# Gate products for eight tokens at a time, gate stores issued by ScalarE, a paired comparison in decoding, and weight tiles that begin 52 bytes in

## The chip, the cores and the metric

The kernel runs on one core of one Trainium2 chip. The metric is the device time of one execution in microseconds (us); a kernel's time is the median over its runs. The core has five engines that work side by side: TensorE (PE; PEld is its loading of weights), VectorE (DVE), ScalarE (ACT), GpSimd (POOL) and SyncE (SP, which only issues transfers here).

## The reference, cut to what matters

The reference is a whole network in fp32, with 256 tokens of 1,024 features. A first block of two layers (SwiGLU, a mixer of three recurrences, SwiGLU) is followed by a second block of two layers (attention, then PEER), with a second stream of 256 context tokens that is needed in its first layer only. PEER is the part that the change touches by its code:

```python
def peer(h, w_q, sub_keys, u, v):            # 8 heads, 128 keys, top 16, 16384 experts
    q = (h @ w_q).reshape(T, 8, 2, 128)
    s = jnp.einsum('thpd,hpnd->thpn', q, sub_keys)
    sv, si = lax.top_k(s, 16)
    cand = (sv[:, :, 0, :, None] + sv[:, :, 1, None, :]).reshape(T, 8, 256)
    fv, fi = lax.top_k(cand, 16)
    i1 = jnp.take_along_axis(si[:, :, 0], fi // 16, axis=-1)
    i2 = jnp.take_along_axis(si[:, :, 1], fi % 16, axis=-1)
    g = jax.nn.softmax(fv, axis=-1)
    # each token: sum over its 128 chosen experts of g * gelu(h . u[i]) * v[i],  i = i1 * 128 + i2
```

It runs three times: on the tokens and on the context in layer 0, and on the tokens in layer 1. Outside of it nearly all the work is matrix products of the 256 tokens with weights.

## The kernel before

**Matrix products.** Every fp32 product is made of three faster ones (mm3, L242): each operand is split into a high part H and a rest L, and H x H, H x L and L x H are added up in PSUM. wsplit (L229) splits each weight tile that a transfer has brought into raw or rawx: split (L214) lets ScalarE copy H (L221), VectorE subtract to L (L224), and GpSimd subtract a share of it (L226). The tiles wh, wl (wxh, wxl, wch, wcl in other pools) are 1,024 + 64 floats long on each partition, and the split weights lie in them from float LEAD on (L220; LEAD is 16, 64 bytes). In the two expert functions it is 0 where the tokens are 512 at a time. The weights are the operand that TensorE loads (128 x 128), the tokens are streamed through (256 columns, or 512).

**PEER.** A sparse choice of experts is computed densely: all 16,384 experts are applied to all tokens, and a gate matrix with zeros for what wasn't chosen multiplies the activations. route_choices makes the queries and the top 16. route_gates (L1330) then works on two blocks of 128 tokens. decode (L1349) turns the 128 choices of each token into key numbers i1 and i2 and gates: it finds the two ranks ra and rb by arithmetic, compares each with 0 to 15 into eq (tag req, L1381, 2,048 elements), multiplies by the list of keys (L1384), adds up in halves (L1386, L1388), and transposes. gates (L1402) builds the matrix: for four tokens VectorE compares key numbers with 0 to 127 into e (g_e, L1412, 1,024 elements) and multiplies its first half by three bf16 parts of the gate into o (g_o, L1416, 1,536 elements); twelve bf16 matmuls fill one PSUM bank r, ScalarE copies it into rst (L1424), and after eight such steps SP issues the store of 2 MB to the DRAM buffer gd (L1425). One place makes 8 stores; there are three places, so 24. g_e and g_o have three buffers each, r has two banks, rst two buffers.

**Around it.** The three places lie beside other work: the context's beside a SwiGLU (about 1270 to 1512 us), the tokens' of layer 0 beside the first nine groups of the context's experts (1820 to 2040), and those of layer 1 beside the first groups of its own experts (3527 to 3709). An expert group is hidden (products with u, GELU, tag act), and some groups later (15 at the third place) down: gated loads the gates back from gd into eG (L1461), VectorE multiplies them into ea (L1465) and splits it (eah, eal), and products with v are added up in acc. Behind the second place the pools change: rawx and wx are opened and the experts run 512 tokens at a time.

**Order.** The order on each engine is fixed when the kernel is built, by a scheduler that goes by its own estimates; on the chip each engine works in that order and waits on semaphores. SP issues the loads of weights and, up to now, the stores of gates, in one order (L197 is a load of raw or rawx).

Of the kernel before, what the change touches and what calls it, by code (L numbers as in the profile page):

```python
# [15 lines left out]
U32 = mybir.dt.uint32  # L16
U8 = mybir.dt.uint8
BF = mybir.dt.bfloat16
AF = mybir.ActivationFunctionType
OP = mybir.AluOpType  # L20
# [9 lines left out]
GD_LEVELS = (2, 4, 8, 16, 32, 64)  # L30
NFIRST = 9

LEAD = 16


TIERS = ((0, 0, 1, 16), (16, 1, 3, 8), (40, 4, 4, 4), (56, 8, 8, 1))
# [72 lines left out]
class Net:  # L109
    def __init__(self, ctx, tc):  # L110
# [9 lines left out]
        self.mod, self.mw = {}, {}  # L120
        self.nsplit, self.share, self.pooled, self.ngap, self.lead = 0, 0, 0, 0, LEAD

# [1207 lines left out]
    def route_gates(self, choices, gd, base, side="left"):  # L1330
        stack, si, fv, fi = choices
        with stack, self.route_pool("b", side) as self.ph, self.psum("routeb", side, r=2):
            self.gb = dict(e=3, o=3)
            iota2 = self.t([128, 128, 2], "iota2", 1, BF)
            self.nc.gpsimd.tensor_copy(iota2, self.c("iota").unsqueeze(2).to_broadcast([128, 128, 2]))
            for tb in range(2):
                jt = self.decode(si[tb], fv[tb], fi[tb])
                self.gates(jt, iota2, gd, base + tb * 4)
# [10 lines left out]
    def decode(self, si, fv, fi):  # L1349


        nc = self.nc
        e = self.t([128, 8, 16], "rge")
        z = self.t([128, 8], "rgz")
        nc.vector.tensor_tensor(e, fv, fv[:, :, 0:1].to_broadcast([128, 8, 16]), OP.subtract)
        nc.scalar.activation(e, e, AF.Exp)
        nc.vector.tensor_reduce(z, e, AX.X, OP.add)
        nc.vector.reciprocal(z, z)
        nc.vector.tensor_tensor(e, e, z.unsqueeze(2).to_broadcast([128, 8, 16]), OP.mult)
        sif = self.t([128, 8, 2, 16], "rsif", 1, BF)  # L1360
        nc.vector.tensor_copy(sif.rearrange("p h a k -> p (h a) k"), si)

        sh = self.t([128, 8, 16], "rsh", 1, U32)
        nc.vector.tensor_scalar(sh, fi, 3, None, OP.logical_shift_right)
        p, ra, rb, x = [self.t([128, 8, 16], f"rr{i}", 1, BF) for i in range(4)]
        nc.vector.tensor_copy(p, fi)
        nc.vector.tensor_scalar(ra, sh, -1.0, 0.0, OP.add, OP.max)
        sh = self.t([128, 8, 16], "rsh", 1, U32)
        nc.vector.tensor_scalar(sh, fi, 2, None, OP.logical_shift_right)
        nc.vector.scalar_tensor_tensor(ra, sh, -6.0, ra, OP.add, OP.max)  # L1370
        nc.vector.scalar_tensor_tensor(ra, p, -48.0, ra, OP.add, OP.max)
        nc.vector.tensor_scalar(x, ra, 8.0, 8.0, OP.mult, OP.add)
        nc.vector.scalar_tensor_tensor(x, ra, 16.0, x, OP.mult, OP.min)
        nc.vector.tensor_scalar(rb, ra, 4.0, 24.0, OP.mult, OP.add)
        nc.vector.tensor_tensor(x, x, rb, OP.min)
        nc.vector.scalar_tensor_tensor(x, ra, 48.0, x, OP.add, OP.min)
        nc.vector.tensor_tensor(rb, p, x, OP.subtract)
        tp = self.bank((128, 3, 128), "r")
        for i, r in enumerate((ra, rb)):
            eq = self.t([128, 128, 16], "req", 1, BF)  # L1380
            nc.vector.tensor_tensor(eq, r.rearrange("p h k -> p (h k)").unsqueeze(2).to_broadcast([128, 128, 16]),  # L1381
                                    self.iota16.unsqueeze(1).to_broadcast([128, 128, 16]), OP.is_equal)
            e4 = eq.rearrange("p (h k) a -> p h k a", h=8)
            nc.vector.tensor_tensor(e4, e4, sif[:, :, i].unsqueeze(2).to_broadcast([128, 8, 16, 16]), OP.mult)  # L1384
            for n in (8, 4, 2):
                nc.vector.tensor_tensor(eq[:, :, 0:n], eq[:, :, 0:n], eq[:, :, n:2 * n], OP.add)  # L1386
            ii = self.t([128, 128], "rii")
            nc.vector.tensor_tensor(ii, eq[:, :, 0], eq[:, :, 1], OP.add)  # L1388
            nc.tensor.transpose(tp[:, i], ii, self.ident)
        nc.tensor.transpose(tp[:, 2], e.rearrange("p h k -> p (h k)"), self.ident)  # L1390
        ji = self.t([128, 64, 2, 2], "rji", 2, BF)
        jg = self.t([128, 64, 3, 2], "rjg", 2, BF)
        nc.scalar.copy(ji.rearrange("p n c t -> p c n t"), tp[:, 0:2].rearrange("p c (n t) -> p c n t", t=2))
        g = tp[:, 2].rearrange("p (n t) -> p n t", t=2)
        nc.vector.tensor_copy(jg[:, :, 0], g)
        g1 = self.t([128, 64, 2], "rg")
        nc.vector.tensor_tensor(g1, g, jg[:, :, 0], OP.subtract)
        nc.vector.tensor_copy(jg[:, :, 1], g1)
        nc.vector.tensor_tensor(jg[:, :, 2], g1, jg[:, :, 1], OP.subtract)
        return ji, jg  # L1400

    def gates(self, j, iota2, gd, base):  # L1402

        nc = self.nc
        ji, jg = j
        for c in range(4):
            st = self.t([128, 128, 32], "rst", 2)
            for q in range(8):
                n0 = c * 16 + q * 2
                e = self.g([128, 2, 2, 128, 2], "e", BF)  # L1410
                o = self.g([128, 2, 3, 128, 2], "o", BF)
                nc.vector.tensor_tensor(e.rearrange("p n c i t -> p (n c) i t"),  # L1412
                                        iota2.unsqueeze(1).to_broadcast([128, 4, 128, 2]),
                                        ji[:, n0:n0 + 2].rearrange("p n c t -> p (n c) t").unsqueeze(2)
                                        .to_broadcast([128, 4, 128, 2]), OP.is_equal)
                nc.vector.tensor_tensor(o, e[:, :, 0:1].to_broadcast([128, 2, 3, 128, 2]),  # L1416
                                        jg[:, n0:n0 + 2].unsqueeze(3).to_broadcast([128, 2, 3, 128, 2]), OP.mult)
                ps = self.bank((128, 4, 128), "r")
                for t in range(4):
                    l, r = e[:, t // 2, 1, :, t % 2], o[:, t // 2, :, :, t % 2]  # L1420
                    for i in range(3):
                        self.mm(ps[:, t], l, r[:, i], t + i == 0, t == 3 and i == 2)
                dst = st.rearrange("p i t -> p t i")[:, q * 4:q * 4 + 4]
                nc.scalar.copy(dst, ps)  # L1424
            nc.sync.dma_start(gd[base + c], st.rearrange("p i t -> p (i t)"))  # L1425

    def experts(self, h, grps, u_d, v_d, gd, f=None, quiet=()):

# [12 lines left out]
        def hidden(grp):  # L1441
            self.lead = 0 if T == 512 else LEAD
            acts[grp] = []
# [26 lines left out]
        def down(grp):  # L1470
            As = gated(grp)
            self.lead = 0 if T == 512 else LEAD
            for half in range(2):
# [28 lines left out]
        for grp in grps[-lag:] if lag else ():  # L1502
            down(grp)
        self.share, self.lead = 0, LEAD
        return acc
# [282 lines left out]
```

## Time and profile before

| | us |
|---|---|
| median of 3 runs | 4281.34 |
| lowest and highest | 4268.89, 4295.14 |
| the profiled execution | 4265.51 |
| its span, first to last instruction | 4263.7 |
| TensorE busy in it | 4092.1 |
| VectorE busy in it | 2884.7 |
| ScalarE busy in it | 1948.4 |
| GpSimd busy in it | 1404.4 |

Busy times are those of the profile's page. Matmuls are pipelined: one of 256 columns lasts about 0.28 us from its start to its modelled end, while the next starts after 0.11 to 0.12 us, so the pace is read from starts, or as a stretch's length divided by its matmuls. The granted clock (PEclk) is a share of full speed. A name such as g_o<-g_e,rjg is the tile written and the tiles read, and L1416 the line of the kernel.

### The profile page before, as it was taken

What the parts mean: (1) busy time and instruction counts of PE and PEld (TensorE: products, weight loads), DVE (VectorE), ACT (ScalarE), POOL (GpSimd) and SP (SyncE); (2) the same over time, 40 slices, a digit from 0 to 9 for tenths busy, and PEclk for the clock granted to TensorE, in tenths of its full rate; (3) what the DMA queues carried; (4) which work ended last, traced back from release to release, by engine and by line L of the source; (5) the groups of instructions that cost most, each with busy time, mean ns of one, the idle gap of its engine ahead of it and who ended that gap; (6) DMA issues with size and microseconds to landing.
All of it is one profiled execution on the core that took longest, in us unless ns stands there. A gap on an engine that the chain in (4) does not pass through costs nothing.

```text
span 4263.7 us, 77051 instructions
## 1 busy us (share of the span) xinstructions
PE 4092.1 (96%) x31290; PEld 3779.8 (89%) x31290; DVE 2884.7 (68%) x5472; ACT 1948.4 (46%) x2711; POOL 1404.4 (33%) x1239
## 2 busy tenths in 40 slices
PE   8999999999999999999899999999999999899999
PEld 8998999998979987999688888888998699799999
DVE  6686757786869966999444444444656789775555
ACT  4462555444535644556332332323444546644443
POOL 5641454555402200420222222222354131005554
PEclk9999999999999989999999999999999999999999
DMA  6545654545365552456434333333464135686654
GB/s 213 179 165 203 228 174 154 187 140 191 135 232 188 208 184 87 169 198 228 168 119 129 113 125 119 124 114 120 162 213 159 74 132 200 250 279 209 216 193 143
DMA packets 174995, 727.43 MB, mean 171 GB/s; under 512 B 12080, under 2 KB 87088, under 8 KB 103856
## 3 DMA queue, kind: packets, MB, share of 16 engines
q1 hardware_dynamic: 174640, 722.52, 48.5%
q8 instruction: 245, 4.01, 0.4%
q14 instruction: 110, 0.90, 0.1%
HBM read 668.99 MB, written 53.48 MB: 169 GB/s over the span
## 4 chain that ended last, share of the span: by engine, by line
PE 83%; DVE 12%; issue 2%; DMA 1%; ACT 1%; POOL 1%; SPq 0%; DVEq 0%; ACTq 0%; POOLq 0%
PE acc L240 29%; PE act L240 23%; PE pj L240 21%; PE r L240 3%; PE gd L240 2%; DVE wl L224 2%; PE s L240 1%; PE hg L240 1%; DVE wcl L224 1%; PE o L240 1%; DVE g_o L1416 1%; PE pt L991 1%; PE at L240 1%; ACT wh L221 1%; DVE g_e L1412 1%
## 5 line engine op out<-in xcount | busy, mean ns | idle before, releaser
L226 POOL TENSOR_TENSOR wl<-raw,wh 128x256 fp32r<-128x256 f32 (+2 forms) x419 | 595.6, 1423 | 1377.2 <-ACT wh L221 1347.1
L221 ACT CAST wh<-raw 128x1024 fp32r<-128x1024 f32 x592 | 620.8, 1051 | 730.5 <-PE acc L240 315.8
L224 DVE TENSOR_TENSOR wl<-raw,wh 128x768 fp32r<-128x768 f32 (+2 forms) x584 | 620.9, 1064 | 475.4 <-ACT wh L221 471.3
L240 PE MATMUL acc<-eah,wl 128*128 128x256 f32 (+1 forms) x1824 | 567.7, 313 | 6.2 <-POOL wl L226 4.3
L240 PE MATMUL acc<-eah,wh 128*128 128x256 f32 (+1 forms) x1824 | 556.8, 312 | 14.9 <-ACT eah L221 14.9
L240 PE MATMUL acc<-eal,wh 128*128 128x256 f32 (+1 forms) x1824 | 568.6, 312 | 0.7 <-DVE eal L224 0.7
L240 PE MATMUL pj<-hH,wh 128*128 128x256 f32 x1776 | 503.3, 284 | 15.7 <-ACT wh L221 12.1
L240 PE MATMUL pj<-hL,wh 128*128 128x256 f32 x1776 | 502.8, 283 | 3.9 <-DVE hL L352 2.5
L240 PE MATMUL pj<-hH,wl 128*128 128x256 f32 x1776 | 502.6, 283 | 1.7 <-DVE wl L224 1.7
L240 PEld LDWEIGHTS acc<-eah,wh 128*128 128x128 f32 x1824 | 344.6, 189 | 36.6 <-ACT eah L221 15.1
L240 PE MATMUL act<-pH,wh 128*128 128x512 f32 (+1 forms) x1056 | 357.6, 339 | 16.1 <-ACT wh L221 12.8
L240 PEld LDWEIGHTS acc<-eah,wl 128*128 128x128 f32 x1824 | 343.6, 189 | 28.6 <-POOL wl L226 4.5
L240 PEld LDWEIGHTS acc<-eal,wh 128*128 128x128 f32 x1824 | 344.4, 189 | 22.5 <-DVE eal L224 1.0
L240 PE MATMUL act<-pH,wl 128*128 128x512 f32 (+1 forms) x1056 | 357.1, 338 | 1.8 <-DVE wl L224 1.8
L240 PE MATMUL act<-pL,wh 128*128 128x512 f32 (+1 forms) x1056 | 357.4, 339 | 0.7 <-DVE pL L334 0.7
L240 PEld LDWEIGHTS pj<-hH,wh 128*128 128x128 f32 x1776 | 338.4, 191 | 21.4 <-ACT wh L221 12.1
L221 ACT CAST wh<-rawx 128x1024 fp32r<-128x1024 f32 x192 | 201.5, 1051 | 337.6 <-PE acc L240 149.9
L224 DVE TENSOR_TENSOR wl<-rawx,wh 128x768 fp32r<-128x768 f32 (+2 forms) x190 | 197.9, 1042 | 219.6 <-ACT wh L221 215.5
L240 PEld LDWEIGHTS pj<-hL,wh 128*128 128x128 f32 x1776 | 338.2, 190 | 7.0 <-DVE hL L352 3.1
L226 POOL TENSOR_TENSOR wl<-rawx,wh 128x256 fp32r<-128x256 f32 (+2 forms) x159 | 227.7, 1433 | 349.4 <-ACT wh L221 345.4
L240 PEld LDWEIGHTS pj<-hH,wl 128*128 128x128 f32 x1776 | 337.1, 190 | 4.2 <-DVE wl L224 2.5
L240 PE MATMUL act<-hH,wl 128*128 128x256 f32 x896 | 251.1, 281 | 5.8 <-POOL wl L226 3.0
(557 smaller groups left out, 11175.3 us busy)
## 6 DMA issues: line engine op xcount, KB each, us to landing
raw<-u SPq DMA_DIRECT2D x114, 1024.0 KB, 4.8
raw<-v SPq DMA_DIRECT2D x104, 1024.0 KB, 4.9
eG<-gd SPq DMA_DIRECT2D x49, 1024.0 KB, 8.7
rawm<-wmod SPq DMA_DIRECT2D x96, 512.0 KB, 5.6
gd<-rst SPq DMA_DIRECT2D x24, 2048.0 KB, 7.2
raw<-f1gu SPq DMA_DIRECT2D x42, 1024.0 KB, 4.8
raw<-f2gu SPq DMA_DIRECT2D x42, 1024.0 KB, 4.9
rawx<-v SPq DMA_DIRECT2D x42, 1024.0 KB, 4.9
```

The lines of the kernel that those rows point to most:

```text
L221: self.nc.scalar.copy(H, src)
L224: self.nc.vector.tensor_tensor(L[..., 0:n], src[..., 0:n], Hf[..., 0:n], OP.subtract)
L226: self.nc.gpsimd.tensor_tensor(L[..., n:], src[..., n:], Hf[..., n:], OP.subtract)
L240: return self.nc.tensor.matmul(out, l, r, start=start, stop=stop)
L991: nc.tensor.transpose(pt[:, kb % 2, qb * 128:(qb + 1) * 128], P[qb][:, kb * 128:(kb + 1) * 128], self.ident)
L1412: nc.vector.tensor_tensor(e.rearrange("p n c i t -> p (n c) i t"), iota2.unsqueeze(1).to_broadcast([128, 4, 128, 2]), ji[:, n0:n0 + 2].rea ...
L1416: nc.vector.tensor_tensor(o, e[:, :, 0:1].to_broadcast([128, 2, 3, 128, 2]), jg[:, n0:n0 + 2].unsqueeze(3).to_broadcast([128, 2, 3, 128, 2 ...
```

## The change

Four things change.

1. gates takes eight tokens at a time: g_e has 2,048 elements and g_o 3,072, and one pair of them feeds two PSUM banks with twelve matmuls each, as before. There are 96 + 96 such products instead of 192 + 192. Their buffers go from three to two, each twice as large, so they take a third more memory.
2. The store of gates is issued from ScalarE's queue instead of SP's.
3. decode compares in pairs: the two ranks are written twice side by side (pairs, 256 elements), and the comparison reads them with a last step of two real elements, where before one element was repeated 16 times. Later steps read every second element of pairs[0]. eq no longer has a tile of its own but takes a buffer of g_e; rii and rg take that of rsh.
4. LEAD is 13 instead of 16: the split weights begin 52 bytes into their tiles. Tiles of 512 tokens at a time keep 0.

```diff
--- before.py
+++ after.py
@@ -30,7 +30,7 @@
 GD_LEVELS = (2, 4, 8, 16, 32, 64)
 NFIRST = 9
 
-LEAD = 16
+LEAD = 13
 
 
 TIERS = ((0, 0, 1, 16), (16, 1, 3, 8), (40, 4, 4, 4), (56, 8, 8, 1))
@@ -1330,7 +1330,7 @@
     def route_gates(self, choices, gd, base, side="left"):
         stack, si, fv, fi = choices
         with stack, self.route_pool("b", side) as self.ph, self.psum("routeb", side, r=2):
-            self.gb = dict(e=3, o=3)
+            self.gb = dict(e=2, o=2)
             iota2 = self.t([128, 128, 2], "iota2", 1, BF)
             self.nc.gpsimd.tensor_copy(iota2, self.c("iota").unsqueeze(2).to_broadcast([128, 128, 2]))
             for tb in range(2):
@@ -1360,31 +1360,37 @@
         sif = self.t([128, 8, 2, 16], "rsif", 1, BF)
         nc.vector.tensor_copy(sif.rearrange("p h a k -> p (h a) k"), si)
 
-        sh = self.t([128, 8, 16], "rsh", 1, U32)
+        p, ra, x = [self.t([128, 128], f"rr{i}", 1, BF) for i in range(3)]
+        pairs = [self.t([128, 128, 2], f"rp{i}", 1, BF) for i in range(2)]
+        fi = fi.rearrange("p h k -> p (h k)")
+        twice = lambda a: a.unsqueeze(2).to_broadcast([128, 128, 2])
+        sh = self.t([128, 128], "rsh", 1, U32)
         nc.vector.tensor_scalar(sh, fi, 3, None, OP.logical_shift_right)
-        p, ra, rb, x = [self.t([128, 8, 16], f"rr{i}", 1, BF) for i in range(4)]
         nc.vector.tensor_copy(p, fi)
         nc.vector.tensor_scalar(ra, sh, -1.0, 0.0, OP.add, OP.max)
-        sh = self.t([128, 8, 16], "rsh", 1, U32)
+        sh = self.t([128, 128], "rsh", 1, U32)
         nc.vector.tensor_scalar(sh, fi, 2, None, OP.logical_shift_right)
         nc.vector.scalar_tensor_tensor(ra, sh, -6.0, ra, OP.add, OP.max)
-        nc.vector.scalar_tensor_tensor(ra, p, -48.0, ra, OP.add, OP.max)
+        nc.vector.scalar_tensor_tensor(pairs[0], twice(p), -48.0, twice(ra), OP.add, OP.max)
+        ra, rb = pairs[0][:, :, 0], ra
         nc.vector.tensor_scalar(x, ra, 8.0, 8.0, OP.mult, OP.add)
         nc.vector.scalar_tensor_tensor(x, ra, 16.0, x, OP.mult, OP.min)
         nc.vector.tensor_scalar(rb, ra, 4.0, 24.0, OP.mult, OP.add)
         nc.vector.tensor_tensor(x, x, rb, OP.min)
         nc.vector.scalar_tensor_tensor(x, ra, 48.0, x, OP.add, OP.min)
-        nc.vector.tensor_tensor(rb, p, x, OP.subtract)
+        nc.vector.tensor_tensor(pairs[1], twice(p), twice(x), OP.subtract)
         tp = self.bank((128, 3, 128), "r")
-        for i, r in enumerate((ra, rb)):
-            eq = self.t([128, 128, 16], "req", 1, BF)
-            nc.vector.tensor_tensor(eq, r.rearrange("p h k -> p (h k)").unsqueeze(2).to_broadcast([128, 128, 16]),
-                                    self.iota16.unsqueeze(1).to_broadcast([128, 128, 16]), OP.is_equal)
+        for i, r in enumerate(pairs):
+            eq = self.g([128, 128, 16], "e", BF)
+            nc.vector.tensor_tensor(eq.rearrange("p n (a t) -> p n a t", t=2),
+                                    r.unsqueeze(2).to_broadcast([128, 128, 8, 2]),
+                                    self.iota16.rearrange("p (a t) -> p a t", t=2).unsqueeze(1)
+                                    .to_broadcast([128, 128, 8, 2]), OP.is_equal)
             e4 = eq.rearrange("p (h k) a -> p h k a", h=8)
             nc.vector.tensor_tensor(e4, e4, sif[:, :, i].unsqueeze(2).to_broadcast([128, 8, 16, 16]), OP.mult)
             for n in (8, 4, 2):
                 nc.vector.tensor_tensor(eq[:, :, 0:n], eq[:, :, 0:n], eq[:, :, n:2 * n], OP.add)
-            ii = self.t([128, 128], "rii")
+            ii = self.t([128, 128], "rsh")
             nc.vector.tensor_tensor(ii, eq[:, :, 0], eq[:, :, 1], OP.add)
             nc.tensor.transpose(tp[:, i], ii, self.ident)
         nc.tensor.transpose(tp[:, 2], e.rearrange("p h k -> p (h k)"), self.ident)
@@ -1393,7 +1399,7 @@
         nc.scalar.copy(ji.rearrange("p n c t -> p c n t"), tp[:, 0:2].rearrange("p c (n t) -> p c n t", t=2))
         g = tp[:, 2].rearrange("p (n t) -> p n t", t=2)
         nc.vector.tensor_copy(jg[:, :, 0], g)
-        g1 = self.t([128, 64, 2], "rg")
+        g1 = self.t([128, 128], "rsh").rearrange("p (n t) -> p n t", t=2)
         nc.vector.tensor_tensor(g1, g, jg[:, :, 0], OP.subtract)
         nc.vector.tensor_copy(jg[:, :, 1], g1)
         nc.vector.tensor_tensor(jg[:, :, 2], g1, jg[:, :, 1], OP.subtract)
@@ -1405,24 +1411,26 @@
         ji, jg = j
         for c in range(4):
             st = self.t([128, 128, 32], "rst", 2)
-            for q in range(8):
-                n0 = c * 16 + q * 2
-                e = self.g([128, 2, 2, 128, 2], "e", BF)
-                o = self.g([128, 2, 3, 128, 2], "o", BF)
+            for q in range(4):
+                n0 = c * 16 + q * 4
+                e = self.g([128, 4, 2, 128, 2], "e", BF)
+                o = self.g([128, 4, 3, 128, 2], "o", BF)
                 nc.vector.tensor_tensor(e.rearrange("p n c i t -> p (n c) i t"),
-                                        iota2.unsqueeze(1).to_broadcast([128, 4, 128, 2]),
-                                        ji[:, n0:n0 + 2].rearrange("p n c t -> p (n c) t").unsqueeze(2)
-                                        .to_broadcast([128, 4, 128, 2]), OP.is_equal)
-                nc.vector.tensor_tensor(o, e[:, :, 0:1].to_broadcast([128, 2, 3, 128, 2]),
-                                        jg[:, n0:n0 + 2].unsqueeze(3).to_broadcast([128, 2, 3, 128, 2]), OP.mult)
-                ps = self.bank((128, 4, 128), "r")
-                for t in range(4):
-                    l, r = e[:, t // 2, 1, :, t % 2], o[:, t // 2, :, :, t % 2]
-                    for i in range(3):
-                        self.mm(ps[:, t], l, r[:, i], t + i == 0, t == 3 and i == 2)
-                dst = st.rearrange("p i t -> p t i")[:, q * 4:q * 4 + 4]
-                nc.scalar.copy(dst, ps)
-            nc.sync.dma_start(gd[base + c], st.rearrange("p i t -> p (i t)"))
+                                        iota2.unsqueeze(1).to_broadcast([128, 8, 128, 2]),
+                                        ji[:, n0:n0 + 4].rearrange("p n c t -> p (n c) t").unsqueeze(2)
+                                        .to_broadcast([128, 8, 128, 2]), OP.is_equal)
+                nc.vector.tensor_tensor(o, e[:, :, 0:1].to_broadcast([128, 4, 3, 128, 2]),
+                                        jg[:, n0:n0 + 4].unsqueeze(3).to_broadcast([128, 4, 3, 128, 2]), OP.mult)
+                for half in range(2):
+                    ps = self.bank((128, 4, 128), "r")
+                    for t in range(4):
+                        n = half * 2 + t // 2
+                        l, r = e[:, n, 1, :, t % 2], o[:, n, :, :, t % 2]
+                        for i in range(3):
+                            self.mm(ps[:, t], l, r[:, i], t + i == 0, t == 3 and i == 2)
+                    t0 = q * 8 + half * 4
+                    nc.scalar.copy(st.rearrange("p i t -> p t i")[:, t0:t0 + 4], ps)
+            nc.scalar.dma_start(gd[base + c], st.rearrange("p i t -> p (i t)"))
 
     def experts(self, h, grps, u_d, v_d, gd, f=None, quiet=()):
 
```

## Rows read from the trace of the kernel before

**Rows 1.** The page: busy time of each engine; the chain's shares by engine.

```profile
PE 4092.1 (96%) x31290; PEld 3779.8 (89%) x31290; DVE 2884.7 (68%) x5472; ACT 1948.4 (46%) x2711; POOL 1404.4 (33%) x1239
...
PE 83%; DVE 12%; issue 2%; DMA 1%; ACT 1%; POOL 1%; SPq 0%; DVEq 0%; ACTq 0%; POOLq 0%
```

**Rows 2.** Stretches: us, busy PE, PEld, DVE, ACT, POOL (instructions); clock, DMA share, GB/s.

```profile
1260.00:1480.00 220.00, 212.13 (x2078) 208.73 (x2077) 205.80 (x309) 130.61 (x159) 51.16 (x21) 0.98 0.55 202
1480.00:1512.00 32.00, 25.81 (x259) 24.27 (x259) 29.45 (x47) 17.60 (x23) 5.75 (x3) 0.89 0.27 99
...
1860.00:2026.00 166.00, 165.56 (x1695) 160.31 (x1694) 154.44 (x205) 112.05 (x120) 2.98 (x2) 1.00 0.60 222
2026.00:2040.00 14.00, 9.28 (x131) 7.50 (x128) 12.41 (x17) 10.89 (x12) 1.81 (x1) 1.00 0.36 152
2040.00:2052.00 12.00, 0.28 (x1) 0.28 (x2) 0.30 (x1) 3.94 (x7) 0.26 (x1) 0.53 0.89 316
...
3540.00:3694.00 154.00, 154.00 (x1635) 152.27 (x1635) 142.64 (x179) 109.14 (x119) 0.00 (x0) 0.99 0.62 228
3694.00:3708.00 14.00, 8.88 (x116) 7.58 (x114) 13.31 (x18) 10.65 (x12) 0.00 (x0) 0.88 0.46 194
3708.00:3724.00 16.00, 1.10 (x8) 0.93 (x5) 3.61 (x9) 3.65 (x6) 0.00 (x0) 0.67 0.75 281
```

**Rows 3.** The chain from 3680 to 3745 us: start, length, what.

```profile
3705.57 0.88 DVE g_o L1416
...
3706.50 0.87 PE r L240 x12
...
3707.39 1.92 ACT rst L1424 x2
...
3709.34 6.26 DMA gd<-rst
...
3715.71 5.88 DMA eG<-gd
```

**Rows 4.** The chain from 2020 to 2072 us.

```profile
2037.74 0.97 DVE g_o L1416
...
2040.70 0.32 SPq L1425
...
2041.06 9.48 DMA rawx<-u
```

**Rows 5.** The tile g_e: duration min/median/max in ns, first and last start, forms.

```profile
L1412 DVE TENSOR_TENSOR g_e<-iota,rji x192: 672/682/1234, 1304.7 to 3704.9; 128x1024 bf16<-128x1024 bf16 x192
L1416 DVE TENSOR_TENSOR g_o<-g_e,rjg x192: 937/950/3147, 1314.4 to 3706.4; 128x1536 bf16<-128x1536 bf16 x192
```

**Rows 6.** The tile req.

```profile
L1381 DVE TENSOR_TENSOR req<-rr,iota x12: 2274/2284/2304, 1272.6 to 3557.7; 128x2048 bf16<-128x2048 bf16 x12
L1384 DVE TENSOR_TENSOR req<-req,rsif x12: 1206/1218/1747, 1276.2 to 3563.3; 128x2048 bf16<-128x2048 bf16 x12
```

**Rows 7.** Groups by line and shape on TensorE: busy us, mean ns, idle before.

```profile
L240 PE MATMUL pj<-hH,wh 128*128 128x256 f32 x1776 | 503.3, 284 | 15.7 <-ACT wh L221 12.1 <-ACT hH L333 2.3 <-DVE gu L378 1.3
...
L240 PE MATMUL pj<-yH,wh 128*128 128x256 f32 x96 | 26.9, 292 | 1.1 <-ACT yH L710 1.1
```

**Rows 8.** Stretches of TensorE alone: us, busy (matmuls), clock, DMA share, GB/s.

```profile
922.00:1008.00 86.00, 86.00 (x733) 1.00 0.51 176
...
3780.00:4200.00 420.00, 420.00 (x3708) 1.00 0.61 208
```

**Rows 9.** The timeline of TensorE from 922 us: start, length, instruction.

```profile
921.78 0.28 PE L240 MATMUL acc<-ffsh,wl 128*128 128x256 f32 x1
...
924.96 0.28 PE L240 MATMUL pj<-hH,wxl 128*128 128x256 f32 x1
```

**Rows 10.** Two lines that load weights from tiles, columns as in rows 5.

```profile
L583 PEld LDWEIGHTS gd<-ccom,g_cv x16: 138/140/145, 270.1 to 1086.3; 128*128 128x128 f32 x16
...
L938 PEld LDWEIGHTS pj<-ccom,mrow x24: 138/141/230, 370.2 to 1266.3; 128*128 128x128 f32 x24
```

## The prediction, made before the changed kernel was run

> **What bounds the kernel now.** I read the page first, then the chain of work that ended last, then three stretches by engine, then single tiles. TensorE is busy 96% of the span, and the chain is 83% TensorE and 12% VectorE [rows 1]. So time falls in two ways only: TensorE's matmuls come closer together, or a hole in its work closes. The change touches both.
>
> The holes it can touch lie at the ends of the three places that build the gate matrix. In the stretches by engine [rows 2] the reader is to see two things for each place. In the long part TensorE is full (165.56 of 166 us, 154.00 of 154) while VectorE is nearly so (154.44, 142.64), so a faster VectorE is worth nothing there by itself. In the short part behind it TensorE starves: at the third place it works 8.88 of 14 us and then 1.10 of 16, so it misses 20.0 us; at the second 9.28 of 14 and 0.28 of 12, 16.4 us missed; at the first 25.81 of 32, and 212.13 of 220 in the part before, 14.1 us missed. The chain says what the third hole waits for [rows 3]: the last g_o, twelve matmuls, the copies, the store of gates (6.26 us), the load back (5.88 us), then ea. All but the first are fixed times behind VectorE's last product. The hole at the second place is another: behind the last g_o the chain passes through the store's issue on SP into the load of rawx, 9.48 us [rows 4].
>
> **VectorE's part.** In gates, g_e with 1,024 elements takes 682 ns and g_o with 1,536 takes 950 (medians of 192) [rows 5]. The doubled forms aren't in the trace. The nearest is the product of 2,048 bf16 elements in decode, 1,218 ns [rows 6]. Two points of one kind, 682 at 1,024 and 1,218 at 2,048, give 0.523 ns per element and 146 ns fixed. So the doubled g_e takes 1,218 (saves 146 for eight tokens) and the doubled g_o 950 + 1,536 x 0.523 = 1,754 (saves 146). A place has 64 pairs now and 32 after: 32 x 292 = 9.3 us saved. From below this could be nothing, if time goes by elements alone; from above it can't exceed the 32 x 2 fixed parts, so 9.3 is also the top.
>
> In decode the comparison of 2,048 elements takes 2,284 ns where the product of the same size takes 1,218 [rows 6]. The two differ in the repeated operand's innermost step, and the change gives the comparison two real values there, as g_e already has (1,024 in 682). I take 1,218: four comparisons a place, 4 x 1,066 = 4.3 us. At worst nothing. Against it, two instructions of each decode write 256 elements instead of 128, and eight read every second value. One such instruction can't cost more than g_e's 682 ns; I take 1 us a place, at most 4.
>
> Sum: 9.3 + 4.3 - 1 = 12.6 us less of VectorE per place. At the third place VectorE's last product opens the chain, so all 12.6 us come off the hole of 20.0 us; TensorE's own work ahead of it stays covered, since 20.0 > 12.6. At the second, 12.6 of 16.4 again. At the first the next stage doesn't wait for the gates: I take half of the 14.1, 7 us (0 to 12.6).
>
> **The store on ScalarE's queue.** SP issues it at 2040.70, after the copy, in 0.32 us, and rawx goes at 2041.06 although the last g_o had ended at 2038.71 [rows 4]. If nothing else held rawx, moving the store frees it up to 2.35 us sooner; I take 1 us. The 24 issues now go to ScalarE, 24 x 0.32 = 7.7 us, in order behind copies that it makes itself, so they wait for nothing foreign; what is queued behind is the next copy or weight split, and ScalarE is busy 46% [rows 1]. Price 0; if the split behind a store is the one that TensorE waits for, 0.32 us each time, at most 7.7. The transfer, 6.26 us at the third place, stays [rows 3].
>
> Gates together: 12.6 + 13.6 + 7 = 33 us, bounds 0 and 50 (20.0 + 16.4 + 14.1).
>
> **Matmul count and buffers.** The twelve matmuls per bank stay, two banks now follow one pair of products. I count no gain for TensorE. Shared buffers are the third rival.
>
> **Weights 52 bytes in.** This touches far more work. 19,752 matmuls of 256 columns take a weight tile that moves (35 groups of the view by shape; first and last in [rows 7]). They run in two rhythms. From 3780 to 4200 us, 3,708 matmuls fill 420 us: 113.3 ns from start to start. From 922 to 1008, 733 fill 86 us, 117.3 [rows 8]; in the timeline of that stretch 28 matmuls run from 921.78 to 924.96, 27 steps of 117.8 ns [rows 9]. The clock is full in both and TensorE never idle, and the two rows are of different forms (acc, pj) at one pitch, so the form isn't the cause. What is left is where operands lie, and the change moves one operand of each pair against the other. Counting start-to-start distances over the whole timeline gives about 6,300 slow ones. All fast: -6,300 x 4.5 ns = -28 us. All slow: 13,450 x 4.5 = +60. A third pitch can't be excluded and no row prices it. Weights that start off a 64-byte step don't show. The nearest is the row of 259 floats in the convolution's tile, whose second half starts 12 bytes off: loading it as weights takes 140 ns (16 times) against 141 for mrow, which is in line [rows 10]. So no cost per load; since the shift is the same for all tiles, I expect one pitch nearly everywhere, and fast is the commoner one (68%).
>
> The Trainium skill, page "SBUF — State Buffer", section "Specifications (TRN2)", speaks against this: it has lines of 16 bytes and a penalty for each access that crosses to a new one. A weight row of 512 bytes covers 32 lines from a 64-byte start and 33 from byte 52, an estimate of 3% more of a load. By it the pairs would all be slow, +60 us; the equal 140 and 141 ns speak for no effect, but of loads in no dense stream.
>
> **The sum.** The profiled execution took 4265.5 us (span 4263.7 and 1.8 around it), 0.37% or 16 us below the median 4281.3 of the runs. 4265.5 - 33 - 28 = 4204.5; on the median's footing 4220.
>
> **Rivals.**
> - B, gates gain, rhythms keep their mix: tiles of activations lie at many places, and a shift may turn as many fast as slow. -33: 4248. For it: both rhythms appear now with all weights at one offset.
> - C, on the other side: every pair takes the slow rhythm, as it does from 922 to 1008 us. -33 + 60 = +27: 4308. It decides once more than 6,300 + 33 / 0.0045 = 13,600 of the 19,752 pairs are slow. For it: 52 is no multiple of 16. Against: [rows 10].
> - D, VectorE's gain doesn't arrive. Two buffers of eight tokens hold less lead than three of four steps do for the order of instructions, and the second decode's comparisons now queue for gate buffers, where they had a tile of their own; behind a waiting comparison stand VectorE's weight splits, for which TensorE waits. The gain of a place, 12.6 us over 32 pairs, is gone at 0.39 us of wait per pair; twelve matmuls take 0.87 us [rows 3], so a wait for one bank would do it. With fast pairs 4253, with the mix as now 4281.
>
> **How the numbers follow.** Rhythm: fast 0.54, as now 0.29, slow 0.17. Gates: arrive 0.82. So the forecast has 0.44, B 0.24, C 0.14, D 0.18 (half of it at 4253, a third at 4281, the rest at 4341). Time 4220. Its own range is 4185 to 4243: below by the bound of 50 us for the gates and by what a profile and a median differ, above by 10 us for the gates. The range for 8 in 10 is 4185 to 4292: forecast, B and most of D, without C. About 1%, 43 us, is what a measurement can tell from no change: faster by more than that means under 4238.5, which is most of the forecast and a fifth of B, 0.48; same holds the rest of B, most of C and of D, 0.45; slower by over 1% is a C without the gates' gain, 0.07.
>
> **What would show it.** Doubled g_e at 1.2 us and g_o at 1.75; the comparison at 1.2 instead of 2.28; the hole before the third load of eG shorter by 12 us; the rawx load at the second place 13 us earlier relative to the start of the gates; 922 to 1008 at 113.3 ns. It is wrong if long stretches show 117.8 ns or more where they had 113.3, or if VectorE waits for TensorE's r over 0.39 us per pair.

## The result, and the profile after

| | us |
|---|---|
| before, median of 4 | 4275.8 (4268.9 to 4295.1) |
| after, median of 4 | 4212.7 (4208.8 to 4222.3) |
| ratio | 0.985, interval 0.982 to 0.988 |
| after, profiled execution and its span | 4208.75, 4206.7 |

The change is 1.5% faster, 63 us by the medians and 57 us from profile to profile. 4220 was forecast. The page after, busy time and the chain's shares by engine, against [rows 1]:

```profile
PE 4071.0 (97%) x31290; PEld 3768.6 (90%) x31290; DVE 2822.1 (67%) x5280; ACT 1943.9 (46%) x2711; POOL 1324.3 (31%) x1239
...
PE 86%; DVE 8%; DMA 2%; ACT 2%; issue 1%; POOL 0%; SPq 0%; DVEq 0%; ACTq 0%; POOLq 0%
```

VectorE is busy 62.6 us less, though the gates and decodings were to give 38, and GpSimd 80 us less, though no line of it was touched. That is the first sign of something that the prediction didn't have.

The new products, as [rows 5] and [rows 6] (ns min/median/max, first and last start):

```profile
L1418 DVE TENSOR_TENSOR g_e<-iota,rji x96: 1202/1219/3018, 1270.7 to 3646.3; 128x2048 bf16<-128x2048 bf16 x96
L1422 DVE TENSOR_TENSOR g_o<-g_e,rjg x96: 1742/1752/2299, 1277.7 to 3647.5; 128x3072 bf16<-128x3072 bf16 x96
...
L1385 DVE TENSOR_TENSOR g_e<-rp,iota x12: 1209/1220/1668, 1248.3 to 3564.0; 128x2048 bf16<-128x2048 bf16 x12
```

Their medians are 1,219, 1,752 and 1,220 ns where 1,218, 1,754 and 1,218 were worked out. The third place's end, chain and stretches as [rows 3] and [rows 2]:

```profile
3647.55 1.77 DVE g_o L1422
...
3649.36 0.88 PE r L240 x12
...
3650.26 1.91 ACT rst L1432 x2
...
3652.19 6.26 DMA gd<-rst
...
3658.58 5.88 DMA eG<-gd
```

```profile
3630.00:3646.00 16.00, 13.44 (x161) 12.94 (x160) 15.24 (x12) 12.30 (x14) 0.00 (x0) 1.00 0.63 226
3646.00:3652.00 6.00, 3.10 (x48) 2.75 (x48) 3.27 (x3) 3.70 (x4) 0.00 (x0) 1.00 0.25 102
3652.00:3668.00 16.00, 1.31 (x5) 1.01 (x5) 4.74 (x11) 3.68 (x6) 0.00 (x0) 0.61 0.82 307
```

The last stretch is as empty as in [rows 2] (1.31 of 16 us against 1.10): the hole that was to lose 12.6 us is still there. TensorE's waits (us in total, times, longest), the kernel before and then the changed one, say it in one line each, and show where a hole did shrink:

```profile
PE acc L240 <- ACT eah L221: 14.9, 1, 14.9
PE act L240 <- ACT wh L221: 12.8, 2, 12.1
```

```profile
PE acc L240 <- ACT eah L221: 15.0, 1, 15.0
...
PE act L240 <- ACT wh L221: 5.5, 2, 4.8
```

The first line of each is the hole behind the third place, the second holds the one behind the second place, where rawx was waited for: 12.1 us became 4.8.

### The profile page after: what moved, and what is told of

The parts are those of the page before. It is cut to its first block, busy times and chain, and to the rows that moved or that the text cites. A ratio compares the mean times of both kernels' runs of the same rounds, so it can differ in the third digit from the quotient of the medians.

```text
span 4206.7 us, 76811 instructions
## 1 busy us (share of the span) xinstructions
PE 4071.0 (97%) x31290; PEld 3768.6 (90%) x31290; DVE 2822.1 (67%) x5280; ACT 1943.9 (46%) x2711; POOL 1324.3 (31%) x1239
## 4 chain that ended last, share of the span: by engine, by line
PE 86%; DVE 8%; DMA 2%; ACT 2%; issue 1%; POOL 0%; SPq 0%; DVEq 0%; ACTq 0%; POOLq 0%
PE acc L240 30%; PE act L240 23%; PE pj L240 23%; PE r L240 3%; PE gd L240 2%; DVE wl L224 2%; PE s L240 1%; PE hg L240 1%; PE o L240 1%; DVE g_cv L435 1%; DMA rawm<-wmod 1%; ACT wh L221 1%; PE pt L991 1%; PE at L240 1%; DVE g_o L1422 0%
## 5 line engine op out<-in xcount | busy, mean ns | idle before, releaser
L226 POOL TENSOR_TENSOR wl<-raw,wh 128x256 fp32r<-128x256 f32 (+2 forms) x419 | 537.7, 1284 | 1421.9 <-ACT wh L221 1381.2
L240 PE MATMUL pj<-hH,wh 128*128 128x256 f32 x1776 | 501.5, 283 | 15.7 <-ACT wh L221 12.1
L240 PEld LDWEIGHTS acc<-eah,wh 128*128 128x128 f32 x1824 | 343.9, 189 | 36.7 <-ACT eah L221 15.2
L240 PEld LDWEIGHTS pj<-hH,wh 128*128 128x128 f32 x1776 | 337.4, 190 | 21.4 <-ACT wh L221 12.1
L226 POOL TENSOR_TENSOR wl<-rawx,wh 128x256 fp32r<-128x256 f32 (+2 forms) x159 | 217.1, 1366 | 345.8 <-ACT wh L221 333.4
L240 PE MATMUL act<-hL,wh 128*128 128x256 f32 x896 | 252.3, 282 | 0.7 <-DVE hL L334 0.7
```

The costliest lines, as they stand in the source:

```text
L226: self.nc.gpsimd.tensor_tensor(L[..., n:], src[..., n:], Hf[..., n:], OP.subtract)
L240: return self.nc.tensor.matmul(out, l, r, start=start, stop=stop)
```

## The experiments

Ratios are to runs of the kernel before in the same session; its medians there were 4273 to 4275 us.

### The two halves of the change

Weights 52 bytes in, alone, in the kernel before:

```diff
-LEAD = 16
+LEAD = 13
```

> The kernel before with weights 52 bytes in and nothing else changed. Theory 1 (both parts pay): up to the first gates, at about 1250 us, the two kernels work in the same order, and the changed one was 25 us earlier there, so this edit alone gives 20 to 30 us: ratio 0.993 to 0.995. Theory 2 (the gates did it all, the 25 us are the spread between executions): ratio 0.998 to 1.002. Theory 3 (more than half is the offset): 35 us or more, ratio under 0.992.

Measured 4241.8, ratio 0.994 (0.992 to 0.997), 24 us. The changed kernel with 64 bytes:

```diff
-LEAD = 13
+LEAD = 16
```

> The changed kernel with weights 64 bytes in, so the gates, the store's queue and the decoding alone. Theory 1: 30 to 38 us faster than before, ratio 0.991 to 0.993, and as many slow pairs (117.8 ns) as before. Theory 2: 57 us or more, ratio under 0.987. Theory 3: 20 us or less, ratio over 0.995.

Measured 4250.5, ratio 0.9925 (0.990 to 0.995), 32 us by the ratio and 23 by the medians. Theory 1 is the nearest, though the medians alone come close to theory 3: the product of the two ratios is 0.987 where the change has 0.985. So both halves have about the size forecast, 28 and 33 us. One sign of theory 1 missed. As many slow pairs as before were expected, and the profiled execution shows some 9,100 against 6,200; its last long stretch ran slow, at 117.7 ns from start to start, of which more below. What follows asks whether they have it for the reasons given.

### Which part of the gates pays

Three runs each put one part into the kernel before, with weights at 64 bytes. The paired comparison is decode as in the change, but with eq in its own tile:

```diff
+        for i, r in enumerate(pairs):
+            eq = self.t([128, 128, 16], "req", 1, BF)
+            nc.vector.tensor_tensor(eq.rearrange("p n (a t) -> p n a t", t=2),
+                                    r.unsqueeze(2).to_broadcast([128, 128, 8, 2]),
...
```

> The kernel before with the paired comparison in decoding alone (in a tile of its own, weights 64 bytes in). Theory P (what pays is TensorE's waits beside the decodings): the comparison falls from 2.28 to 1.22 us, the waits for weight splits at the three decodings (4.4, 4.3 and 3.3 us in the kernel before) go, and the time falls by 8 to 12 us although VectorE saves 4.3 us a place only. Theory Q (what pays is VectorE's saving, carried to the last gate): 4 us a place where the end waits for it, 8 us at most, and the holes behind the last gates shrink by 4 us each.

Measured 4268.9, ratio 0.9989 (0.997 to 1.001). The wait for wxl fell from 4.4 to 1.1 us and that for GpSimd's wl at the third place (3.0) went, but the one at the second place stayed (4.3 to 3.2), and the median gives 5 us of the 8 to 12 expected. The holes behind the last gates stayed at 12.1 and 15.0 us, which is against theory Q. The waits are theory P's in part; the gain in time can't be told from nothing.

Eight tokens a step is gates as in the change, but stored by SP, and the old comparison in a buffer of g_e:

```diff
-            self.gb = dict(e=3, o=3)
+            self.gb = dict(e=2, o=2)
...
-            eq = self.t([128, 128, 16], "req", 1, BF)
+            eq = self.g([128, 128, 16], "e", BF)
```

> The kernel before with eight tokens a step (two buffers, the decoding's comparison in a buffer of g_e, but the comparison itself as before, stores from SP). Theory Q: 9.3 us a place off the holes at the second and third place, 20 us or more. Theory P: TensorE is full until shortly before the last gates, so that only its waits for g_o and splits just ahead of them can go: 5 us a place at most, 5 to 15 in all, with the 15 us hole behind the third place's last gates as long as before.

Measured 4265.6, ratio 0.9986 (0.997 to 1.001), 9 us by the medians. TensorE's wait at the third place's hole is 15.2 us. Theory Q's 20 us are out; P's 5 to 15 fit, and so would nothing at all.

The store from ScalarE:

```diff
-            nc.sync.dma_start(gd[base + c], st.rearrange("p i t -> p (i t)"))
+            nc.scalar.dma_start(gd[base + c], st.rearrange("p i t -> p (i t)"))
```

> The kernel before with the store issued by ScalarE alone. Forecast: the load of rawx at the second place goes up to 2.4 us sooner, the hole of 12.1 us there falls to about 10, nothing else: 0 to 3 us, not to be told from none. A rival: SP no longer stands behind the stores (it waited 170 us for copies there), so the loads of weights come sooner all through the three places: 5 us or more, and the hole at the second place falls to about 5 us as it did in the changed kernel (4.8).

Measured 4265.9, ratio 0.9985 (0.996 to 1.001), 8 us by the medians. Here the profile is clearer than the time. SP's timeline, before and in this run (start, length, what):

```profile
2016.24 24.78 SPq L1425 DMA_DIRECT2D gd<-rst  x3
2041.06 0.43 SPq L197 DMA_DIRECT2D rawx<-u  x1
```

```profile
2056.23 0.33 SPq L197 DMA_DIRECT2D rawx<-u  x1
```

and this run's chain:

```profile
2056.24 0.97 DVE g_o L1416
...
2061.49 1.07 ACT wh L221
2062.61 13.90 PE act L240 x48
```

From the last g_o to TensorE's next product it is 6.4 us here, and 14.0 before (2037.74 in [rows 4] to 2051.72). Of the 7.6 us gained, 3.3 are the load's issue: it leaves with the last g_o's start, not 3.3 us behind it. The other 4.3 are its transfer, which is 9.48 us in [rows 4], where it ran together with the store of 2 MB, and at most 5.3 here, where it starts 3 us ahead of it (2056.23 to the copy at 2061.49). That the store slowed it is read from these two transfers; no run tried it by itself. TensorE's wait there is 4.5 us, and 4.8 in the changed kernel. So the forecast of 10 us for this hole missed, and the rival's 5 us is what came.

The three parts make 0.40% together, the half as a whole 0.75% with an interval of 0.3 to either side; whether something is gained only together stays open.

### What the weights' offset does

A pair is a weight load and its matmul of 256 columns. Its pitch is the time from one matmul's start to the next one's: pairs near 113.3 ns are called fast, those of 116 ns and more slow.

Only the rests moved, then only the high parts, both in the kernel before:

```diff
-            H, L = [self.t([128, shape[1] + 64], tag + i, bufs, F32R, pool)[:, lead:lead + shape[1]] for i in "hl"]
+            H, L = [self.t([128, shape[1] + 64], tag + i, bufs, F32R, pool)[:, x:x + shape[1]]
+                    for i, x in (("h", lead), ("l", lead - 3 if lead else 0))]
```

> The kernel before with the high parts 64 bytes in and the rests 52. GpSimd's subtraction writes the rests; it took 1,507 ns at 64, 48 and 96 bytes and 1,415 at 52. If its gain hangs on where it writes, it is 1,415 here too, and the stretch before the first gates where VectorE is full (820 to 922 us) shortens as with 52 bytes throughout: 10 us or so. If it hangs on the distance between what it reads and writes in several tiles, it is neither. Of TensorE's pairs a third takes rests: if each pair's pitch goes by its own operands, the share of slow pairs lies between that of the two kernels, nearer the one with 64 bytes; if by the sequence of two loads, a new pitch shows in streams that alternate.

```diff
+                    for i, x in (("h", lead - 3 if lead else 0), ("l", lead))]
```

> The kernel before with the high parts 52 bytes in and the rests 64, the mirror of the run before. GpSimd's subtraction stayed at 1,513 ns where only the rests moved, so if it is the place of the high part that it reads, it takes 1,415 here. Theory G (the 10 us of the stretch from 820 to 1020 come from GpSimd and through it VectorE): that stretch is 8 to 11 us shorter here, as with 52 bytes throughout, and the time falls by 10 to 20 us. Theory T (they come from TensorE's pitch): it shortens only as the pitch of its pairs does, and GpSimd's duration is no matter.

Rests alone: 4266.9, ratio 0.998 (0.996 to 1.000). High parts alone: 4246.6, ratio 0.995 (0.993 to 0.9965), as good as both together (0.994). GpSimd's subtraction in the tile wl, in the kernel before, with the rests moved, with the high parts moved:

```profile
L226 POOL TENSOR_TENSOR wl<-raw,wh x419: 728/1507/9643, 12.1 to 4234.4; 128x256 fp32r<-128x256 f32 x119, 128x384 fp32r<-128x384 f32 x17, 128x1024 fp32r<-128x1024 f32 x4
```

```profile
L227 POOL TENSOR_TENSOR wl<-raw,wh x419: 731/1513/9617, 12.2 to 4234.8; 128x256 fp32r<-128x256 f32 x119, 128x384 fp32r<-128x384 f32 x17, 128x1024 fp32r<-128x1024 f32 x4
```

```profile
L227 POOL TENSOR_TENSOR wl<-raw,wh x419: 631/1412/9551, 12.3 to 4210.4; 128x256 fp32r<-128x256 f32 x119, 128x384 fp32r<-128x384 f32 x17, 128x1024 fp32r<-128x1024 f32 x4
```

So it is the place of the high part that GpSimd reads, 52 bytes into its tile, that saves it 95 ns, and not the place that it writes. The run with the rests moved has some 3,400 slow pairs, fewer than with nothing moved (6,200) or both (4,100), which none of its theories had. Part of how GpSimd's gain reaches the end of the kernel shows in the stretch from 820 to 1020 us, where the context's top 16 keep VectorE full. Its subtraction for wcl and GpSimd's beside it (busy us, mean ns), in the same three kernels:

```profile
L224 DVE TENSOR_TENSOR wcl<-rawc,wch 128x256 fp32r<-128x256 f32 x13 | 18.4, 1415 | 0.8 <-ACT wch L221 0.6
...
L226 POOL TENSOR_TENSOR wcl<-rawc,wch 128x768 fp32r<-128x768 f32 x13 | 24.3, 1869 | 0.0
```

```profile
L225 DVE TENSOR_TENSOR wcl<-rawc,wch 128x256 fp32r<-128x256 f32 x14 | 18.4, 1312 | 0.6 <-ACT wch L222 0.5
...
L227 POOL TENSOR_TENSOR wcl<-rawc,wch 128x768 fp32r<-128x768 f32 x14 | 26.0, 1860 | 0.0
```

```profile
L225 DVE TENSOR_TENSOR wcl<-rawc,wch 128x256 fp32r<-128x256 f32 x13 | 14.8, 1139 | 0.7 <-ACT wch L222 0.6
...
L227 POOL TENSOR_TENSOR wcl<-rawc,wch 128x768 fp32r<-128x768 f32 x13 | 20.4, 1573 | 0.0
```

With the high parts moved GpSimd's falls by 296 ns, and VectorE's, a third as many elements on another engine, by 276. (With the rests moved VectorE's mean of 1,312 counts one more, short, product; its busy time is the same 18.4 us.) VectorE reads the moved high part too, but by itself that doesn't make it faster. Its products of 1,024 elements, in which GpSimd has no share, before and in the changed kernel:

```profile
L224 DVE TENSOR_TENSOR wl<-raw,wh 128x1024 fp32r<-128x1024 f32 x173 | 210.6, 1219 | 68.9 <-ACT wh L221 66.5 <-PE pt L991 2.2
```

```profile
L224 DVE TENSOR_TENSOR wl<-raw,wh 128x1024 fp32r<-128x1024 f32 x173 | 211.2, 1224 | 65.3 <-ACT wh L221 62.1 <-PE pt L991 2.3
```

So VectorE gains where GpSimd works beside it. In the stretch TensorE's wait for the scores' copy (rsc) goes from 4.3 us to 1.4. Its length can be read between two marks, GpSimd's first rcd and the last transpose of the convolution (first and last start):

```profile
L1323 POOL TENSOR_TENSOR rcd<-rsv x192: 201/214/1299, 843.5 to 3511.7; 128x16 f32<-128x16 f32 x96, 128x24 f32<-128x24 f32 x48, 128x8 f32<-128x8 f32 x48
```

```profile
L584 PEld LDWEIGHTS gd<-ccom,g_cv x16: 138/141/143, 270.5 to 1092.4; 128*128 128x128 f32 x16
...
L1324 POOL TENSOR_TENSOR rcd<-rsv x192: 201/215/1302, 848.9 to 3515.1; 128x16 f32<-128x16 f32 x96, 128x24 f32<-128x24 f32 x48, 128x8 f32<-128x8 f32 x48
```

```profile
L584 PEld LDWEIGHTS gd<-ccom,g_cv x16: 137/140/143, 267.7 to 1067.2; 128*128 128x128 f32 x16
...
L1324 POOL TENSOR_TENSOR rcd<-rsv x192: 201/214/1300, 834.7 to 3486.3; 128x16 f32<-128x16 f32 x96, 128x24 f32<-128x24 f32 x48, 128x8 f32<-128x8 f32 x48
```

843.5 to 1086.3 ([rows 10]) is 242.8 us; with the rests moved 243.5, with the high parts moved 232.5; with both moved 235.1, and in the changed kernel 231.6. The runs with all weights at 64 bytes have 239.1 to 243.4 and those with the high parts at 52 have 231.6 to 235.1, so executions differ by 4 us here, and the gain is 8 us by the means. With one tile moved nearly every pair there is fast, in both kernels (their slow pairs cost 0.6 and 1.2 us in that stretch, 6.4 in the kernel before), so the 11 us between them aren't TensorE's pitch; and the rests alone took 5.8 us of slow pairs away without making the stretch shorter. Theory G holds for this stretch. Of the 23 us that high parts alone bring from profile to profile, 10.3 lie there, 8.8 before it and 4 behind it. For the 8.8 us the slow pairs give 4.2 and TensorE's waits 3.8; what shortened these waits stays open.

Four other offsets in the changed kernel, LEAD 12 as shown, and then 24, 15 and 29:

```diff
-LEAD = 13
+LEAD = 12
```

> The changed kernel with weights 48 bytes in: a multiple of 16 but not of 64. If a start inside a 16-byte line is what sets the slow pairs' pitch (119.6 ns in the changed kernel, 117.8 before), they come back to 117.8 here. If only the distance from a 64-byte step matters, this behaves as 52 bytes does: ratio near 0.985. If 64-byte steps are no matter at all: as the run with 64 bytes, 0.991 to 0.993.

> The changed kernel with weights 96 bytes in: half a 64-byte step off, so the weights' starts stand against the tokens' tiles the other way round. If the pitch depends on the difference of the two starts at that grain, fast and slow pairs swap for many stages, and the time is over that of the run with 64 bytes by up to 30 us or under it by as much; if it depends on fine misalignment only, the time is that of the run with 64 bytes.

> The changed kernel with weights 60 bytes in, which is off every 8-byte step as 52 is. If a start off the 16-byte steps is what makes the pairs mostly fast and GpSimd 1,415 ns: as with 52 bytes, ratio 0.983 to 0.988. If it is the distance from the tokens' 64-byte steps (48 and 96 bytes were slow in nearly every pair, 64 in a third of them): 60 lies near 64 and the ratio is 0.990 to 0.994.

> The changed kernel with weights 116 bytes in, 64 more than 52. If the place within a 64-byte step decides: the same pitches and time as with 52 bytes, ratio 0.983 to 0.988. If a longer step decides (128 bytes): other pitches, with a ratio that may lie on either side of 0.9925.

| LEAD (bytes) | us | ratio to before | GpSimd, median ns |
|---|---|---|---|
| 13 (52) | 4212.7 | 0.985 (0.982 to 0.988) | 1415 |
| 16 (64) | 4250.5 | 0.9925 (0.990 to 0.995) | 1509 |
| 12 (48) | 4300.6 | 1.0055 (1.0035 to 1.0075) | 1511 |
| 24 (96) | 4297.4 | 1.004 (1.002 to 1.006) | 1510 |
| 15 (60) | 4314.9 | 1.012 (1.009 to 1.014) | 1508 |
| 29 (116) | 4291.4 | 1.005 (1.003 to 1.008) | 1413 |

The last long stretch of experts shows the pitch: TensorE is full in all of them, so length by matmuls is the distance from start to start (us, busy, matmuls, clock, DMA share, GB/s). LEAD 13, 16, 12, 24, 15 and 29 in turn:

```profile
3700.00:4100.00 400.00, 400.00 (x3532) 1.00 0.63 218
```

```profile
3790.00:4190.00 400.00, 400.00 (x3398) 1.00 0.58 200
```

```profile
3850.00:4200.00 350.00, 350.00 (x2974) 1.00 0.59 201
```

```profile
3850.00:4200.00 350.00, 350.00 (x2952) 1.00 0.58 197
```

```profile
3850.00:4200.00 350.00, 350.00 (x2932) 1.00 0.57 196
```

```profile
3850.00:4200.00 350.00, 350.00 (x2942) 1.00 0.58 198
```

113.3, 117.7, 117.7, 118.6, 119.4 and 119.0 ns; at 64 bytes the same stretch has 113.3 in [rows 8]. Of the forecasts for these four, none had the time, but for the last one's second theory, which left it open. No theory on a grain holds: 48 is a multiple of 16 and slow, 60 lies off 16 and is slower, and 116, which stands in its 64 bytes where 52 does, keeps GpSimd fast and TensorE slow. What the pairs need from a start can't be said from six values.

The stage of 512 tokens with the offset too:

```diff
-            self.lead = 0 if T == 512 else LEAD
+            self.lead = LEAD
```

> The changed kernel with 52 bytes in the stage of 512 tokens too (4,416 matmuls of 512 columns, 226.7 ns each from start to start with weights at 0). If the pitch there is set by the 512 columns alone, nothing: ratio as the changed kernel, 0.985. If the longer loads show, some 2 to 6 ns more a pair, 9 to 26 us slower. If weights at 0 had cost something: up to 10 us faster.

Measured 4245.1, ratio 0.995 (0.992 to 0.998), so 1% slower than the changed kernel. The stage in this run and in the changed kernel:

```profile
2100.00:2900.00 800.00, 800.00 (x3430) 1.00 0.36 117
```

```profile
2060.00:2860.00 800.00, 800.00 (x3531) 1.00 0.37 121
```

233.2 ns a pair against 226.6: 6.6 ns by 4,416 pairs is 29 us, which is the difference of the medians (32). Weights at 52 bytes are not better as such.

No kernel of these beats the changed one. No run has the high parts at 52 bytes and the rests at another place in it.

## Why the prediction was right, and where not

The time, 4212.7, lies 7 us under the forecast and in its own range. The sum's two terms came out near their size: 33 us forecast for the gates, 23 to 32 measured alone; 28 for the offset, 24 measured. Step by step it is less good, and that the sum came out is in part luck: the term for the third place and the reason for the offset's gain failed, and effects that the sum didn't have made up for them.

- **VectorE's durations** were right to 2 ns, by a line through two rows of the same kind.
- **The third place** failed: 12.6 us off the hole, "all", since VectorE's last product opens the chain. It does, but in the chain after, from 3600 to 3640 us, TensorE's expert products and gate matmuls alternate without a pause:

```profile
3635.63 1.39 PE r L240 x24
3637.02 2.81 PE act L240 x24
3639.83 0.72 PE r L240 x12
```

  The order is fixed, so the last gates can't come before the work that stands ahead of them. Before, the chain runs mainly over VectorE from 3676.5 us to the last gates, 30 us; after, for the last 9. So VectorE's saving arrived, but TensorE had work in most of that time. The place's gate matmuls take no less time from first to last than before (148.5 us, and 155.6 after):

```profile
L240 PE MATMUL r<-g_o,g_e x768: 217/218/313, 3559.5 to 3708.0; 128*128 128x128 bf16 x192
```

```profile
L240 PE MATMUL r<-g_o,g_e x768: 217/218/233, 3495.1 to 3650.7; 128*128 128x128 bf16 x192
```

  The hole behind them is the store and the load back, 6.26 and 5.88 us as in [rows 3], and it is as long as before (15.0 us). The prediction counted the whole missed 20.0 us as cover; what VectorE could give back was only TensorE's waits ahead of the last gates. From 3500 us to the hole's end they were 4.9 for g_o, 3.0 and 2.7 for splits; after, 4.4 and 1.2. That is about 5 us:

```profile
PE r L240 <- DVE g_o L1416: 4.9, 5, 2.1
PE act L240 <- POOL wl L226: 3.0, 1, 3.0
PE act L240 <- DVE wl L224: 2.7, 3, 1.4
```

```profile
PE r L240 <- DVE g_o L1422: 4.4, 3, 2.6
PE act L240 <- DVE wl L224: 1.2, 1, 1.2
```

  By the starts of the same matmuls of TensorE's order in the two traces, the gates alone shorten the stretch from 3500 to 3730 us by 7.9 us, where 12.6 were forecast.
- **The second place** gave its hole's share, but by another term. The store's queue was priced at 1 us (0 to 2.35); moving it alone gave 7.6. The issue's delay was bounded at 2.35 and measured 3.3, the transfer beside a store of 2 MB wasn't considered. The sign given for this place, the load of rawx 13 us earlier relative to the start of the gates, didn't come: it is 181 us behind the first g_e before (1860.1 to 2041.1) and after (1817.0 to 1997.9). By the same starts the gates alone shorten 1820 to 2075 us by 13.2 us, where 13.6 were forecast.
- **The first place**: 7 us forecast. By the same starts the gates alone shorten 1262 to 1530 us by 6.1 us, and 4 of it is the wait for wxl, 4.4 us before and 0.4 there. The half taken for this place was a guess that came out.
- **TensorE's changes of kind** were counted as nothing. The gate matmuls stand in 141 bursts in the timeline before and in 91 after; each burst costs about 0.09 us over its matmuls and the products beside it (24 products between two bursts take 2.81 us in the chain above, and 24 times 113.3 ns is 2.72), so some 5 us.
- **The offset** is right in size, and its mechanism didn't show. The forecast was all pairs fast, -28 us. The timeline after has fewer slow pairs, 4,500 and not 6,200, but they stand 119.6 ns apart and not 117.9: their excess over 113.3 is about 28.7 us after (27 to 32 by where the count is cut off) and 28.5 before, so the pitch gave nothing between these two executions. The "one pitch nearly everywhere" that the prediction expected didn't come, though its sign of 922 to 1008 us did (656 matmuls in the 74 us from 907 us after); and some 2,500 pairs that were fast before became slow, such as 508 in the 60 us from 1700 us after, at 118.1 ns. With the offset alone, matmul by matmul in the same order, 3 of the 28 us from profile to profile lie in distances between matmuls that follow without a pause, and the rest in longer ones, most of them waits. What came is GpSimd's subtraction, 95 ns faster, and through VectorE's shorter one the stretch from 820 to 1020 us; that is shown for 8 to 10 us there, and for the other waits it is not shown. Nor is the pitch out of the medians: with all weights at 64 bytes the last long stretch ran slow in two of five profiled executions (the gates alone, the store alone), 18 us each, and at 52 bytes in none of three. These are too few to tell its share of the 24 us. The prediction had weighed the offset on TensorE only; ScalarE, VectorE and GpSimd read and write the same tiles.
- **Rival C** didn't happen at 52 bytes, but its mechanism is real: at 48, 60, 96 and 116 bytes the second place's hole is as short as in the changed kernel (4.8 us) and the pairs go slow nearly everywhere, and the time is 0.4 to 1.2% over before. Its 4308 us is near the 4291 to 4315 measured there. By the line rule of the Trainium skill ("SBUF — State Buffer", "Specifications (TRN2)"), as the prediction read it, 48 bytes should have been as good as 64 and 52 worse than both; the runs have 48 slow and 52 the best.
- **Rival D**: VectorE's g_e waited for TensorE's r for 6.4 us in the whole kernel, 0.07 us a pair where 0.39 would have undone the gain. Two buffers are enough here:

```profile
DVE g_e L1418 <- PE r L240: 6.4, 6, 2.8
```

## To carry to other kernels

A hole behind a fixed chain of store and load can't be shortened by the engine ahead of it when the waiting engine's own fixed order is full until then: count what that engine waits before the hole, not the hole. When a tile's place in memory changes, list every engine that reads or writes it, and look for the engine that is full in some stretch, before pricing the largest one. And try an offset on the chip: six values spread over 2.4% here, without a rule that would have picked the best.

## What the runs showed that was not expected

- A GpSimd subtraction of fp32 took 1,412 to 1,415 ns with one of its read operands 52 or 116 bytes into the tile, and 1,507 to 1,513 ns at 48, 60, 64 and 96.
- VectorE's subtraction beside it shortened by nearly as many ns as GpSimd's own (276 and 296), and not where GpSimd had no share (1,219 and 1,224).
- Which of two pitches a long stretch of matmuls takes seems not to be fixed by the weights' offset or the kernel, though no kernel has two traces. In the run that moved only the store, the profiled execution had the last 540 us at 117.8 ns (3,399 matmuls in the 400 us from 3800 us) and took 4293.6 us, where its median is 4265.9; in the kernel before, [rows 8], the same stretch ran at 113.3. 4,450 pairs by 4.5 ns are 20 us, most of the 28 us by which this execution lies over its median.
- A load of 1 MB took 9.5 us beside a store of 2 MB, and at most 5.3 us ahead of it.
